# The first mixer's residual: raw rows turned again, or normed rows kept and scaled back

## The chip, the cores and the metric

The kernel runs on one core of a Trainium2 chip. Its engines are TensorE (PE, with its weight loads as PEld), VectorE (DVE), ScalarE (ACT), GpSimd (POOL) and SyncE (SP), which here only issues DMAs. The metric is the device time of one execution in microseconds.

## The reference

The program is one inference step of a two-layer decoder for a prompt of 1024 tokens and 8 single sample tokens, with model width 1024. What matters here is the start of layer 0, for `h = x`:

```python
hn = rmsnorm(h, g[0])                 # y = h * rsqrt(mean(h*h) + EPS), then y * g
mix, S = a_mixer(hn, w_in_a[l], ...)  # gated recurrence and attention into 256 memory tokens
h = h + rmsnorm(mix, g[1])            # the residual: h is still x here
h = h + rmsnorm(swiglu(rmsnorm(h, g[2]), w_gu[l], w_down[l]), g[3])
```

The memory tokens (256 x 1024) are projected to keys and values for both layers, which the attention part of each mixer reads and which are outputs too.

## The kernel before

The kernel works on features in partitions and tokens along the free dimension. The 1024 features are 8 blocks of 128 (`ND = 8`); the tokens are two groups, `g = 0` with 512 prompt tokens and `g = 1` with the other 512 and the 8 sample tokens (520 wide). Every projection (`proj`, matmuls at L220) is an fp32 product made from three fp32r products: weights are loaded by SP (L201), split into a high part on ACT (L206) and a low part on DVE (L207), and multiplied with inputs that were split in the same way. Raw weight tiles have 5 buffers, split ones 5; a projection needs two of each.

**The order of the work.** The code is written as generators. `weave` interleaves several of them by step counts and weights, `drain` runs one to its end; this gives the order in which instructions are written down. A planner then orders each engine's queue by that order and by its own estimate of when operands and buffers are ready. On the chip each engine, and each DMA queue, works through its own list in order: an instruction that waits holds up all behind it.

**Input norm, `start` (L326), called for both groups.** `rms_rows` (L313) takes 128 token rows at a time (tokens in partitions): a sum of squares on ACT or DVE, a logarithm (L320) and an exponential (L321) give `1/rms` per token, and DVE scales the rows in place (L322). Then, for each feature block, PE transposes four 128x128 pieces into one PSUM bank (L349), and ACT and DVE evacuate it into the two parts of the input `x` with the gain column `g[0]` (L352, L353). Even blocks use the bank `ns`, of which there is one, odd blocks `s`, of which there are three. The unscaled rows `x` aren't kept.

**Residual, `residual` (L365).** It adds `h` to the normed mixer output `R`, with DVE's scalar_tensor_tensor (L381) and an add. For later sub-layers `h` comes from a DRAM scratch `hs[g]`, which the residual before it stored at L389. For the first mixer (`first=True`) there is no such store: it loads the raw rows of `x_prompt` again (L372), PE turns them in the bank `ns` (L380), and DVE adds the bank (L383); sample tokens are added from `xsraw` (L385). The first group's residual runs among the second group's projections (`weave` at L1547), the second group's among the heads of layer 1 (L1572).

**The memory tokens, `mem_load` (L798).** Two loads (L803), 16 transposes in the bank `ns` (L807), and copies and subtractions (L227, L228) into the tiles `memt`. `mem_keys` (L824) and `mem_values` (L851) read them. All three are one chain, woven with the first mixer's core (`hgrn_prompt`, first matmuls at L1168) at L1536 to L1539; before that, at L1535, the first mixer's projections for values, gate and queries run alone.

**Small pools.** `T()` gives 128x520 tiles of pool `t`, three buffers, used by the silu, the gate projection, key copies and the masks at the start. `B()` gives 128x512 tiles, seven buffers. A buffer is free again when its last reader has finished; where that is a DMA, when the DMA has landed.

Of the kernel before, what the change touches and what calls it, by code (L numbers as in the profile page):

```python
# [18 lines left out]
P = 128  # L19
# [4 lines left out]
def tile_decoder(  # L24
# [73 lines left out]
    def NS():  # L98
        return nsp.tile([P, 512], F32, tag="ns", name=nm("ns"))
# [74 lines left out]
    def chain(*gens):  # L174
        for g_ in gens:
            yield from g_
# [133 lines left out]
    def wo_tiles(g):  # L310
        return [X(g) for _ in range(ND)]

    def rms_rows(xt, n, dve=False):  # L313
        ss = small([P, 1], tag="rr")
        junk = M().rearrange("p a n -> p (a n)")[:n, :D]
        if dve:
            nc.vector.tensor_tensor_reduce(junk, xt, xt, 1.0, 0.0, ALU.mult, ALU.add, ss[:n])
        else:
            nc.scalar.activation(junk, xt, AF.Square, accum_out=ss[:n])
        nc.scalar.activation(ss[:n], ss[:n], AF.Ln, scale=1.0 / D, bias=epsb[:n])  # L320
        nc.scalar.activation(ss[:n], ss[:n], AF.Exp, scale=-0.5)  # L321
        nc.vector.tensor_scalar(xt, xt, ss[:n], None, op0=ALU.mult)  # L322

# [2 lines left out]
    def start(g, out):  # L326
# [4 lines left out]
            xs = C().rearrange("p a n -> p (a n)")[:NB]  # L331
            nc.sync.dma_start(xs, x_sample.rearrange("b o d -> (b o) d"))
        for tb in range(CH):
            rms_rows(xtok[g][:, tb, :], P, g == 0 and tb % 2 == 1)
            yield
        if g:
            ps = S()
# [8 lines left out]
        for k in range(ND):  # L346
            ps = S() if k % 2 else NS()
            for tb in range(CH):
# [4 lines left out]
            made[0] = nc.vector.scalar_tensor_tensor(  # L353
                x[:, 1, :G], ps, gk, x[:, 0, :G].bitcast(F32), op0=ALU.mult, op1=ALU.subtract
            )
            if g:
                pk = pn[:, k * NB : (k + 1) * NB]
                nc.scalar.activation(x[:, 0, G:], pk, AF.Copy, scale=gk)
                nc.vector.scalar_tensor_tensor(
                    x[:, 1, G:], pk, gk, x[:, 0, G:].bitcast(F32), op0=ALU.mult, op1=ALU.subtract  # L360
                )
# [2 lines left out]

    def residual(g, R, rstd, gc, store, acc=None, first=False):  # L365
        n = NG[g]
        w = D // 2 if first else n
        ht = [xpool.tile([P, 2, w], F32, tag=f"x{g}", name=nm("ht")) for _ in range(ND // 2)]
        for j in range(ND // 2):
            if first:  # L370
                t0 = g * G + j * P
                nc.sync.dma_start(ht[j].rearrange("p a n -> p (a n)"), x_prompt[0, t0 : t0 + P, :])  # L372
            else:
                nc.sync.dma_start(ht[j], hs[g][:, 2 * j : 2 * j + 2, :n])
        for k in range(ND):
            if first:
                ps = NS()
                for tb in range(CH):
                    xf = ht[tb].rearrange("p a n -> p (a n)")
                    nc.tensor.transpose(ps[:, tb * P : (tb + 1) * P], xf[:, k * P : (k + 1) * P], ident)  # L380
            nc.vector.scalar_tensor_tensor(R[k][:, :n], R[k][:, :n], gc(k), rstd[:, :n], op0=ALU.mult, op1=ALU.mult)  # L381
            if first:
                nc.vector.tensor_add(R[k][:, :G], R[k][:, :G], ps)  # L383
                if g:
                    nc.vector.tensor_add(R[k][:, G:n], R[k][:, G:n], xsraw[:, k, :])  # L385
            else:
                nc.vector.tensor_add(R[k][:, :n], R[k][:, :n], ht[k // 2][:, k % 2, :])
            if store:
                nc.sync.dma_start(hs[g][:, k, :n], R[k][:, :n])  # L389
            if acc is not None:  # L390
                sq_acc(acc, R[k][:, :n], k, n)
            yield
# [1082 lines left out]
    with tc.issue_after(made[0].ins):  # L1475
# [56 lines left out]
        nc.gpsimd.tensor_tensor(pidx, pidx, iot, op=ALU.add)  # L1532
    drain(head)
    a0 = mixer_a(0, x0)
    drain(a0.v(), a0.fq())  # L1535
    weave(  # L1536
        (a0.core(), 22),
        (chain(mem_load(), mem_keys(0), mem_values(0), mem_keys(1), mem_values(1), a0.qm(M)), 22),
    )  # L1539
    a0.open()  # L1540
    a1 = mixer_a(1, x1)
# [94 lines left out]
```

## Time and profile before

| | |
|---|---|
| median of 3 runs | 2454.28 us (2452.27 to 2455.25) |
| profiled execution | 2454.5 us |
| its span | 2452.8 us |
| PE busy | 2413.3 us (98%) |
| DVE busy | 1639.9 us (67%) |
| ACT busy | 1252.4 us (51%) |
| POOL busy | 187.0 us (8%) |
| DMA moved | 397.40 MB, 162 GB/s in the mean |

Busy times are sums of instructions' spans with overlaps counted once. In a timeline a row is a run of like instructions: its start, its length, the engine, the line of the code, what it writes and reads, and in brackets how long the engine stood idle before it and what ended that. In a table by stretches each engine's busy time stands with its count of instructions, then the clock granted to PE, the share of time in which the 16 DMA engines were busy, and what they moved.

### The profile page before, as it was taken

The page shows a single profiled execution, that of the slowest core. Times are in us where ns is not written, and L with a number is a line of the kernel's source. Part 1 is how long each engine was busy: PE and PEld are TensorE (multiplying, and loading weights), DVE is VectorE, ACT ScalarE, POOL GpSimd, SP SyncE. Part 2 cuts the span into 40 slices and gives each one's busy share as a digit, 9 for nine tenths or more (in the row PEclk, how much of TensorE's full clock was granted, in tenths as well). Part 3 has the DMA queues.
Part 4 walks back from the last instruction along what each step waited for, and adds up shares of the span by engine and source line. Part 5 has one row for each costly group of instructions (what it writes and reads, how often), then busy time and mean ns, then how long its engine had stood idle before and what let it go on. Part 6 is the DMA issues. An engine that isn't in the chain of part 4 may idle for free.

```text
span 2452.8 us, 42098 instructions
## 1 busy us (share of the span) xinstructions
PE 2413.3 (98%) x15839; PEld 2161.2 (88%) x15839; DVE 1639.9 (67%) x2987; ACT 1252.4 (51%) x2441; POOL 187.0 (8%) x315
## 2 busy tenths in 40 slices
PE   8999999999999999999999999999999999999998
PEld 6888889888879988999999989877777888999998
DVE  5766557665797686664756685788688467755565
ACT  5547644354445554555434554555554445654445
POOL 1000101111000000111200102121000100000000
PEclk9999999999999999999999999999999999999999
DMA  6354676567645447676766649745354563464542
GB/s 190 100 174 110 157 197 161 135 171 204 204 137 166 132 147 235 176 188 161 190 172 168 199 132 291 206 146 154 95 164 120 145 191 116 144 194 141 151 143 74
DMA packets 534733, 397.40 MB, mean 162 GB/s; under 512 B 21325, under 2 KB 473018, under 8 KB 534530
## 3 DMA queue, kind: packets, MB, share of 16 engines
q1 hardware_dynamic: 505346, 315.02, 43.2%
q0 software_dynamic: 29184, 79.70, 14.2%
q8 instruction: 124, 2.03, 0.3%
q14 instruction: 79, 0.65, 0.1%
HBM read 364.81 MB, written 101.14 MB: 190 GB/s over the span
## 4 chain that ended last, share of the span: by engine, by line
PE 84%; DVE 6%; DMA 5%; issue 2%; ACT 2%; POOL 0%; SPq 0%; DVEq 0%; ACTq 0%; POOLq 0%
PE mm L220 44%; PE q L511 13%; PE q L648 9%; PE q L464 3%; PE mm L1042 2%; PE s L1188 1%; DMA c<-in_cache_mem_v 1%; PE s L1385 1%; PE s L906 1%; PE mm L824 1%; PE mm L851 1%; PE q L680 1%; PE s L1351 1%; PE s L875 1%; DVE ws L207 1%
## 5 line engine op out<-in xcount | busy, mean ns | idle before, releaser
L220 PE MATMUL mm<-x,ws 128*128 128x260 f32 (+1 forms) x6240 | 1113.6, 335 | 4.9 <-DVE t L237 1.7
L220 PEld LDWEIGHTS mm<-x,ws 128*128 128x128 f32 x6240 | 941.8, 188 | 125.8 <-issue 2.4
L206 ACT CAST ws<-w 128x512 fp32r<-128x512 f32 (+1 forms) x652 | 382.3, 588 | 489.5 <-PE mm L220 337.0
L207 DVE TENSOR_TENSOR ws<-w,ws 128x512 fp32r<-128x512 f32 (+1 forms) x652 | 418.9, 648 | 246.8 <-ACT ws L206 241.7
L220 PE MATMUL mm<-m,ws 128*128 128x512 f32 (+1 forms) x1344 | 281.8, 361 | 0.1
L220 PEld LDWEIGHTS mm<-m,ws 128*128 128x128 f32 x1344 | 217.9, 189 | 36.8 <-issue 1.0
L648 PE MATMUL q<-m,ws 128*128 128x260 f32 (+1 forms) x1824 | 221.8, 283 | 0.0
L648 PEld LDWEIGHTS q<-m,ws 128*128 128x128 f32 x1824 | 218.9, 188 | 1.2 <-DVE t L534 0.4
L502 DVE TENSOR_TENSOR ws<-w,ws 128x512 fp32r<-128x512 f32 x181 | 124.0, 690 | 86.6 <-ACT ws L501 83.6
L501 ACT CAST ws<-w 128x512 fp32r<-128x512 f32 x181 | 111.8, 621 | 110.2 <-PE q L648 35.6
L511 PE MATMUL q<-x,ws 128*128 128x260 f32 (+1 forms) x1188 | 158.1, 282 | 0.0
L511 PEld LDWEIGHTS q<-x,ws 128*128 128x128 f32 x1188 | 148.7, 188 | 0.0
L511 PE MATMUL q<-y,ws 128*128 128x260 f32 x912 | 119.7, 284 | 0.4 <-ACT q L521 0.3
L511 PEld LDWEIGHTS q<-y,ws 128*128 128x128 f32 x912 | 113.7, 189 | 0.8 <-ACT q L521 0.5
L464 PE MATMUL q<-x,ws 128*128 128x260 f32 (+1 forms) x720 | 91.3, 284 | 0.2 <-DVE r L400 0.2
L464 PEld LDWEIGHTS q<-x,ws 128*128 128x128 f32 x720 | 88.4, 189 | 1.8 <-DVE r L400 0.5
L511 PE MATMUL q<-a,ws 128*128 128x260 f32 (+1 forms) x672 | 87.0, 282 | 0.0
L511 PEld LDWEIGHTS q<-a,ws 128*128 128x128 f32 x672 | 83.2, 188 | 0.0
L657 DVE TENSOR_TENSOR r<-r,q 128x260 f32<-128x260 f32 (+1 forms) x128 | 48.5, 420 | 50.5 <-PE q L648 50.5
L237 DVE TENSOR_SCALAR t<-mm 128x512 f32<-128x512 f32 (+1 forms) x58 | 40.1, 691 | 48.0 <-PE mm L220 47.8
L563 POOL COPY mk<-a 128x1 f32<-128x1 f32 x36 | 21.3, 592 | 645.5 <-ACT a L1241 392.9
L228 DVE TENSOR_TENSOR m<-t,m 128x512 fp32r<-128x512 f32 (+1 forms) x88 | 60.8, 691 | 9.4 <-ACT m L227 8.7
(355 smaller groups left out, 3029.5 us busy)
## 6 DMA issues: line engine op xcount, KB each, us to landing
w<-in_w_gu SPq DMA_DIRECT2D x297, 256.0 KB
w<-in_w_down SPq DMA_DIRECT2D x160, 256.0 KB
wsum<-in_w_gu POOLq DMA_DIRECT2D x72, 512.0 KB, 6.6
w<-wsum SPq DMA_DIRECT2D x104, 256.0 KB
w<-in_w_in_a SPq DMA_DIRECT2D x80, 256.0 KB
w<-in_w_o SPq DMA_DIRECT2D x64, 256.0 KB
wsum<-in_w_gu POOLq DMA_DIRECT2D x24, 640.0 KB, 7.3
wsum<-wsum POOLq DMA_DIRECT2D x24, 512.0 KB, 5.7
```

The source lines that it names most:

```text
L206: nc.scalar.copy(ws[:, 0, :n, :], raw[:, :n, :])
L207: nc.vector.tensor_sub(ws[:, 1, :n, :], raw[:, :n, :], ws[:, 0, :n, :].bitcast(F32))
L220: nc.tensor.matmul(ps[:, a, : PW[g]], wt, xt[k][:, xi, o : o + PW[g]], start=(k == 0 and wi == 0), stop=(k == nk - 1 and wi == 2),)
L228: nc.vector.tensor_sub(dst[1], src, dst[0].bitcast(F32))
L237: nc.vector.tensor_scalar(sv(x, g), pv(ps, g), -44.0, None, op0=ALU.max)
L464: ins = nc.tensor.matmul(pp[a][:, :h], wt, xt[k][:, xi, a * h : (a + 1) * h], start=(k == 0 and wi == 0), stop=(k == ND - 1 and wi == 2),)
L501: nc.scalar.copy(w[:, 0, :], src)
L502: nc.vector.tensor_sub(w[:, 1, :], src, w[:, 0, :].bitcast(F32))
L511: nc.tensor.matmul(ps[:, :h], w[:, wj, k * P : (k + 1) * P], x[:, xi, :], start=(first and k == 0 and wi == 0), stop=(k == 3 and wi == 2), ...
L648: nc.tensor.matmul(pp[a][:, :h], wt, mids[k][:, xi, a * h : (a + 1) * h], start=(k == 0 and wi == 0), stop=(k == nf - 1 and wi == 2),)
L657: nc.vector.tensor_add(d, d, pp[a][:, :h])
L1042: nc.tensor.matmul(pb[i][:, a, :], xt[k][:, xi, c * P : (c + 1) * P], ws[:, s, :], start=(k == 0 and wi == 0), stop=(k == ND - 1 and wi == 2),
```

## The change

The first mixer's residual no longer turns the raw rows. `start` keeps what it has in PSUM anyway, the turned rows scaled by `1/rms` but without the gain: ACT copies each bank to a tile of pool `t` and SP stores it to `hs[g]`. `rms_rows` makes a second exponential with the sign turned, which is `rms` per token, and SP stores that to a new DRAM scratch `inv[g]`. The residual loads `hs[g]` as later residuals do, loads `inv[g]` broadcast over the partitions, multiplies each block by it on DVE, and adds. Sample tokens are added as before. The loads from `x_prompt` and the transposes at L380 are gone.

Besides, `mem_load` is taken out of the chain beside the core and woven with the first mixer's gate and query projections; the weight of the chain that is left goes from 22 to 20.

```diff
-    def rms_rows(xt, n, dve=False):
+    inv = [tc.dram_tile([1, G], F32, name=f"inv{g}") for g in range(2)]
+
+    def rms_rows(xt, n, dve=False, keep=None):
...
         nc.scalar.activation(ss[:n], ss[:n], AF.Ln, scale=1.0 / D, bias=epsb[:n])
+        if keep is not None:
+            si = small([P, 1], tag="ri")
+            nc.scalar.activation(si, ss, AF.Exp, scale=0.5)
+            nc.sync.dma_start(keep, si)
         nc.scalar.activation(ss[:n], ss[:n], AF.Exp, scale=-0.5)
...
         for tb in range(CH):
-            rms_rows(xtok[g][:, tb, :], P, g == 0 and tb % 2 == 1)
+            rms_rows(
+                xtok[g][:, tb, :], P, g == 0 and tb % 2 == 1,
+                inv[g][:, tb * P : (tb + 1) * P].rearrange("o p -> p o"),
+            )
...
                 x[:, 1, :G], ps, gk, x[:, 0, :G].bitcast(F32), op0=ALU.mult, op1=ALU.subtract
             )
+            t = T()
+            nc.scalar.copy(t[:, :G], ps)
+            nc.sync.dma_start(hs[g][:, k, :G], t[:, :G])
...
     def residual(g, R, rstd, gc, store, acc=None, first=False):
         n = NG[g]
-        w = D // 2 if first else n
+        w = G if first else n
         ht = [xpool.tile([P, 2, w], F32, tag=f"x{g}", name=nm("ht")) for _ in range(ND // 2)]
         for j in range(ND // 2):
+            nc.sync.dma_start(ht[j], hs[g][:, 2 * j : 2 * j + 2, :w])
+        if first:
+            iv = B()
+            nc.sync.dma_start(iv, inv[g].rearrange("o n -> (o n)").partition_broadcast(P))
+        for k in range(ND):
+            h = ht[k // 2][:, k % 2, :]
             if first:
-                t0 = g * G + j * P
-                nc.sync.dma_start(ht[j].rearrange("p a n -> p (a n)"), x_prompt[0, t0 : t0 + P, :])
-            else:
-                nc.sync.dma_start(ht[j], hs[g][:, 2 * j : 2 * j + 2, :n])
-        for k in range(ND):
-            if first:
-                ps = NS()
-                for tb in range(CH):
-                    xf = ht[tb].rearrange("p a n -> p (a n)")
-                    nc.tensor.transpose(ps[:, tb * P : (tb + 1) * P], xf[:, k * P : (k + 1) * P], ident)
+                nc.vector.tensor_mul(h, h, iv)
             nc.vector.scalar_tensor_tensor(R[k][:, :n], R[k][:, :n], gc(k), rstd[:, :n], op0=ALU.mult, op1=ALU.mult)
-            if first:
-                nc.vector.tensor_add(R[k][:, :G], R[k][:, :G], ps)
-                if g:
-                    nc.vector.tensor_add(R[k][:, G:n], R[k][:, G:n], xsraw[:, k, :])
-            else:
-                nc.vector.tensor_add(R[k][:, :n], R[k][:, :n], ht[k // 2][:, k % 2, :])
+            nc.vector.tensor_add(R[k][:, :w], R[k][:, :w], h)
+            if first and g:
+                nc.vector.tensor_add(R[k][:, G:n], R[k][:, G:n], xsraw[:, k, :])
...
     a0 = mixer_a(0, x0)
-    drain(a0.v(), a0.fq())
+    drain(a0.v())
+    weave((a0.fq(), 8), (mem_load(), 2))
     weave(
         (a0.core(), 22),
-        (chain(mem_load(), mem_keys(0), mem_values(0), mem_keys(1), mem_values(1), a0.qm(M)), 22),
+        (chain(mem_keys(0), mem_values(0), mem_keys(1), mem_values(1), a0.qm(M)), 20),
     )
```

## The prediction

> **What bounds the kernel now.** I read the page first: the busy shares, then the chain that ended last.
>
> ```profile
> span 2452.8 us, 42098 instructions
> ...
> PE 2413.3 (98%) x15839; PEld 2161.2 (88%) x15839; DVE 1639.9 (67%) x2987; ACT 1252.4 (51%) x2441; POOL 187.0 (8%) x315
> ...
> PE 84%; DVE 6%; DMA 5%; issue 2%; ACT 2%; POOL 0%; SPq 0%; DVEq 0%; ACTq 0%; POOLq 0%
> ```
>
> TensorE is busy 2413.3 of 2452.8 us and carries 84% of the chain. A change can therefore earn in two ways only: it takes instructions out of PE's stream where that stream is dense, or it fills one of the holes, 2452.8 - 2413.3 = 39.5 us in all. Anything added to another engine costs nothing until PE waits for it. The profiled execution took 2454.5 us (span 2452.8 and 1.7 around it), 0.2 above the median of the runs, 2454.28; the sum below is made against 2454.5.
>
> Next I asked for the busy time of each engine in the stretches that the change touches: the first mixer's input norm (two rows), its core's beginning, the second token group's input norm (two rows), and the two residuals (344 to 371, and 960 to 980).
>
> ```profile
> core 0: us, PE busy (x) PEld busy (x) DVE busy (x) ACT busy (x) POOL busy (x), PEclk, DMA share, GB/s
> ...
> 10.00:15.00 5.00, 4.34 (x23) 4.04 (x24) 3.41 (x12) 3.69 (x9) 2.50 (x10) 1.00 0.98 306
> 15.00:20.00 5.00, 4.45 (x25) 3.12 (x24) 5.00 (x15) 3.87 (x8) 0.49 (x3) 1.00 0.43 155
> ...
> 216.00:224.00 8.00, 8.00 (x50) 6.54 (x50) 6.52 (x13) 5.74 (x12) 0.00 (x0) 1.00 0.23 68
> 224.00:232.00 8.00, 7.99 (x65) 7.54 (x64) 7.54 (x16) 7.43 (x18) 1.19 (x4) 1.00 0.24 69
> 344.00:371.00 27.00, 26.98 (x223) 26.14 (x224) 21.48 (x37) 13.71 (x27) 0.00 (x0) 1.00 0.54 167
> ```
>
> ```profile
> 20.00:85.00 65.00, 65.00 (x287) 52.96 (x285) 37.84 (x61) 36.39 (x62) 0.00 (x0) 1.00 0.48 142
> 85.00:95.00 10.00, 6.09 (x30) 5.17 (x29) 7.96 (x22) 5.12 (x16) 0.00 (x0) 0.83 0.10 28
> ...
> 960.00:980.00 20.00, 20.00 (x100) 15.83 (x99) 16.90 (x31) 10.67 (x19) 1.10 (x2) 1.00 1.06 297
> ```
>
> PE is dense in both residuals and from 20 to 85. The one large hole here is 85 to 95: 10.00 - 6.09 = 3.9 us without PE work, at a mean granted clock of 0.83.
>
> **Part 1, the residual's transposes go (gain).** `residual(first=True)` turns raw rows on PE, 4 transposes per feature block, 8 blocks, twice: 64.
>
> ```profile
> L380 PE MATMUL ns<-ident,ht x64: 270/273/329, 343.9 to 974.3; 128*128 128x128 f32 x64
> ```
>
> ```profile
> 355.31 0.60 PE L380 MATMUL ns<-ident,ht 128*128 128x128 f32 x4
> 355.66 4.80 PE L220 MATMUL mm<-x,ws 128*128 128x260 f32 x38
> ...
> 973.94 0.60 PE L380 MATMUL ns<-ident,ht 128*128 128x128 f32 x4
> 974.30 3.25 PE L220 MATMUL mm<-x,ws 128*128 128x512 f32 x13
> ```
>
> One lasts 273 ns, but they overlap. What a group of four displaces is the time from its start to the next projection's first matmul: 0.35 and 0.36 us here. 16 groups x 0.36 = 5.8 us, which I take. The bounds: 0, if the residual becomes limited by DVE instead (part 2), and 64 x 273 ns = 17.5 us if each stood alone. The row is nearest to 5.8, since projections follow without a gap. The Trainium skill, "TensorE: Matmul & The Clock Gate", Part 4: PE-mode transpose, puts a 128x128 transpose at about 275 ns in a kernel's context; the duration agrees with the row of 273, and by that price the sum would gain 17.6 instead of 5.8. That alternative is priced among the rivals from the row alone.
>
> **Part 2, the residual's work on DVE (cost 0).** Per block it gains one multiply of 128x512 with the broadcast inverse; the add reads SBUF instead of PSUM at the same price.
>
> ```profile
> L387 DVE TENSOR_TENSOR r<-r,ht x24: 679/688/695, 862.2 to 2111.2; 128x512 f32<-128x512 f32 x16, 128x520 f32<-128x520 f32 x8
> ```
>
> 8 x 0.69 = 5.5 us a residual. DVE idles 27.00 - 21.48 = 5.5 us from 344 to 371, and the multiplies depend on loads alone, so some can run before the residual's own chain begins at 344. The weight splits queued behind them on DVE have several tiles in hand (five split buffers, two to a projection), so PE should not see it: 0, with 0 to 2 us a residual as bounds. The four loads per residual keep their bytes (512 KB each); they read the scratch `hs` instead of `x_prompt`. Two broadcasts of the inverse are added to SP, under the cover of projections that need no load at that moment.
>
> **Part 3, the memory tokens move (gain).** `mem_load` issues two loads, 16 transposes, 8 ACT copies and 8 DVE subtractions. It moves from the mixer's core into the projections before it.
>
> ```profile
> 84.57 0.60 PE L807 MATMUL ns<-ident,c 128*128 128x128 f32 x4
> 87.77 0.63 PE L807 MATMUL ns<-ident,c 128*128 128x128 f32 x4 [2.60 <-DVE memt L228]
> 89.06 2.93 PE L1168 MATMUL s<-b,a 128*128 128x192 f32 x8 [0.66 <-ACT b L1164]
> 91.78 0.78 PE L807 MATMUL ns<-ident,c 128*128 128x128 f32 x4
> 93.02 0.51 PE L824 MATMUL mm<-memt,ws 128*128 128x256 f32 x2 [0.46 <-ACT memt L227]
> 93.72 1.22 PE L824 MATMUL mm<-memt,ws 128*128 128x256 f32 x8 [0.19 <-DVE memt L228]
> ```
>
> The idle times in the brackets are the hole: 2.60 + 0.66 + 0.46 + 0.19 = 3.9 us. The single bank `ns` makes each group of four wait for the last one's copy and subtraction, and both engines are at the same time on the core's first levels; the memory keys (L824), which are PE's only other work, wait for `memt`. With `memt` ready earlier the keys fill that time. The 16 transposes themselves cost the same in either place. Around them, from 20 to 85, ACT is busy 36.39 of 65 and DVE 37.84, so the moved copies and subtractions are covered by about 27 us of slack on each: 0 there. SP already issues the two loads at 10 us, ahead of everything they could delay:
>
> ```profile
> 10.39 0.91 SPq L803 DMA_DIRECT2D c<-in_mem_prompt  x2
> ```
>  I take the whole 3.9; the bounds are 0 (the hole is the core's own chain) and 3.9.
>
> **Part 4, the first input norm (cost).** Per row block ACT gets one 128x1 exponential and SP one store of 128 single values; per feature block ACT gets one 128x512 copy from PSUM and SP one store of 256 KB.
>
> ```profile
> 8.90 0.20 ACT L321 ACTIVATE rr<-rr 128x1 f32<-128x1 f32 x1
> ...
> 11.92 0.69 ACT L352 ACTIVATE x<-ns,par 128x512 fp32r<-128x512 f32 x1 [0.27 <-PE ns L349]
> ...
> 20.23 0.68 ACT L352 ACTIVATE x<-s,par 128x512 fp32r<-128x512 f32 x1
> ...
> 327.66 0.59 ACT L398 COPY m<-mm 128x512 f32<-128x512 f32 x1 [2.15 <-PE mm L220]
> ```
>
> ```profile
> 19.36 19.71 PE L1042 MATMUL mm<-ws,x 128*128 128x512 f32 x84
> ```
>
> Eight copies are 8 x 0.59 = 4.7 us on ACT. From 10 to 20 ACT has 10.00 - 3.69 - 3.87 = 2.4 us free, and PE is filled to 4.34 and 4.45 of 5. The exponentials lie on the chain to the first transposes: one or two of 0.20 count, 0.3 us. A copy also holds its PSUM bank, and for even blocks that is the single `ns`, so the next blocks come later. But the projection that follows takes 12 matmuls per block at 19.71 / 84 = 0.235 us, 2.8 us a block, while the blocks are now made in (20.23 - 11.92) / 7 = 1.2 us each; only the first two or three can be late. I take 1.2, with bounds 0.2 and 4.7. SP's stores wait for ACT's copies and stand ahead of weight loads; the five raw weight tiles hold that off for a few blocks of 2.8 us.
>
> **Part 5, the second input norm (cost).** The same eight copies, here among the gate's silu and the first projections of the second group. From 216 to 232 ACT is free for 16.00 - 5.74 - 7.43 = 2.8 us, so 4.7 overflows by 1.9. PE starts a projection on a block as soon as that is made, in short runs between the transposes, and can take matmuls of a second projection meanwhile, if its weights are split; that splitting is on ACT too.
>
> ```profile
> 226.13 1.09 PE L220 MATMUL mm<-x,ws 128*128 128x260 f32 x7
> 227.05 0.60 PE L349 MATMUL ns<-ident,xtok 128*128 128x128 f32 x4
> 227.41 1.20 PE L220 MATMUL mm<-x,ws 128*128 128x260 f32 x8
> ```
>
> I take 1.5, with bounds 0 and 4.7. The four exponentials lie under a projection: 0.
>
> **The sum.** 2454.5 - 5.8 - 3.9 + 0 + 1.2 + 1.5 = 2447.5 us, 0.3% under the time before. 0.2%, 4.9 us, is about what a measurement of this kernel can tell from no change.
>
> **Rivals.**
>
> Slower: the `t` slots. The copies go to pool `t`, three buffers, and each is held until its store has landed. Copy 4 waits for slot 1, copy 7 again, so the eight need two holds h; ACT stands at the waiting copy, and behind it in its queue the next block and the weight splits. At the six blocks' own pace, 6 x 1.25 = 7.5 us, nothing is lost; each norm loses 2h - 7.5 beyond. The trace doesn't show a `t` store's landing. The nearest bounds:
>
> ```profile
> 17.98 0.33 SPq L1034 DMA_DIRECT2D w<-in_w_in_a  x1
> ...
> 20.80 0.62 ACT L1036 CAST ws<-w 128x512 fp32r<-128x512 f32 x1
> ```
>
> ```profile
> wsum<-in_w_gu POOLq DMA_DIRECT2D x18, 512.0 KB, 6.2
> ```
>
> A 256 KB load is in use 2.8 us after its issue: h = 0.6 + 2.8 = 3.4, no loss. A transfer of twice the size on POOL's queue lands after 6.2: h = 6.8, 6.1 us lost in each norm, and 2447.5 + 12.2 = 2459.7. It ends slower than before from 2 x (2h - 7.5) = 6.8 on, h = 5.5. Against it: the load is the nearer row, and from 216 on DMA is only 0.23 busy; for it: 0.98 from 10 to 15. The Trainium skill, "DMA: Bandwidth & Descriptors", Anatomy of one DMA, gives about 2.0 us plus bytes over 436 GB/s for a transfer, an estimate of 2.6 us for 256 KB; that too would make this rival harmless, and the load's row agrees with it.
>
> Same: the gains are given back. The hole at 85 stays because DVE, 7.96 of 10 busy, runs the core's own first levels there, and the two norms cost their ACT time at nearly full price: 2454.5 - 5.8 - 1 + 2 + 3 = 2452.7.
>
> Much faster: the transposes cost PE their full duration. Then part 1 earns 64 x 273 ns = 17.5 us and the sum is 2435.8. Against it stand the starts 0.35 us apart per group of four.
>
> **How the numbers follow.** The forecast 0.54 (its own range 2444 to 2450), given back 0.26 (2450 to 2456), `t` slots 0.15 (2457 to 2462), full price of transposes 0.05. Faster by over 0.2%: the forecast without its slowest part, and the last, 0.56. Slower by over 0.2%: 0.15, the `t` slots. The same: the rest, 0.29. The range 2442 to 2457.5 leaves out the full price, most of the `t` slots, and little else. The best of the bounds, 2454.5 - 9.7 = 2444.8 with losses at zero, is inside.
>
> **What would show it.** Right: no transposes in the residual and its projections closing up by 0.36 us a group; from 85 to 95 PE near full with memory keys, at full clock; ACT without waits for a DMA at the new copies; PE's idle time near 10 to 20 up by about 1 us. Wrong: ACT rows at the new copy that wait for a store on `hs`, PE waiting for input blocks at 14 to 30 or at 225 to 240, PE waits on weight splits inside the residuals, or a new hole where the core begins.

## The result and the profile after

The changed kernel is slower: 2477.38 us in the median (2476.06 to 2478.34), against 2455.08 for the kernel before in the same series; the ratio is 1.0091, with a 95% interval of 1.0078 to 1.0104. Forecast were 2447.5 us. The profiled execution took 2478.34 us. The page of the changed kernel, the lines that answer to those of before:

```profile
span 2476.6 us, 42097 instructions
...
PE 2415.2 (98%) x15775; PEld 2160.0 (87%) x15775; DVE 1648.0 (67%) x3003; ACT 1259.2 (51%) x2465; POOL 191.3 (8%) x315
...
PE 83%; DVE 6%; DMA 5%; ACT 3%; issue 2%; POOL 0%; SPq 0%; DVEq 0%; ACTq 0%; POOLq 0%
```

PE has the 64 instructions less, yet its holes grew from 39.5 to 2476.6 - 2415.2 = 61.4 us. To place them, I took landmarks that both kernels have. The rows below are of the view of one line's instructions; the two times after the durations are the first and the last start. First the kernel before:

```profile
L220 PE MATMUL mm<-x,ws x6240: 277/286/802, 38.9 to 2052.4; 128*128 128x260 f32 x107, 128*128 128x512 f32 x88
L339 PE MATMUL s<-ident,c x8: 201/202/223, 216.1 to 216.5; 8*128 8x8 f32 x8
L1022 PE MATMUL s<-ident,t x16: 272/273/329, 346.6 to 368.8; 128*128 128x128 f32 x16
L1188 PE MATMUL s<-a,a x384: 217/263/274, 102.8 to 485.5; 128*126 128x64 f32 x32, 128*124 128x64 f32 x32, 128*120 128x64 f32 x32, 128*112 128x64 f32 x32
L1042 PE MATMUL mm<-ws,x x192: 387/394/502, 14.2 to 941.8; 128*128 128x512 f32 x192
L1351 PE MATMUL s<-a,a x96: 273/539/697, 997.6 to 1831.7; 128*128 128x512 f32 x48, 128*128 128x128 f32 x16, 128*128 128x384 f32 x16, 128*128 128x256 f32 x16
L680 PE MATMUL q<-m,ws x192: 275/283/388, 2415.7 to 2442.9; 128*128 128x264 f32 x96, 128*128 128x256 f32 x96
```

The same instructions in the changed kernel:

```profile
L220 PE MATMUL mm<-x,ws x6240: 277/286/799, 51.4 to 2075.0; 128*128 128x260 f32 x107, 128*128 128x512 f32 x88
L348 PE MATMUL s<-ident,c x8: 201/202/223, 222.1 to 222.6; 8*128 8x8 f32 x8
L1028 PE MATMUL s<-ident,t x16: 272/273/331, 365.6 to 385.1; 128*128 128x128 f32 x16
L1194 PE MATMUL s<-a,a x384: 217/262/273, 115.2 to 501.1; 128*126 128x64 f32 x32, 128*124 128x64 f32 x32, 128*120 128x64 f32 x32, 128*112 128x64 f32 x32
L1048 PE MATMUL mm<-ws,x x192: 387/394/796, 25.6 to 957.5; 128*128 128x512 f32 x192
L1357 PE MATMUL s<-a,a x96: 273/590/847, 1016.4 to 1855.0; 128*128 128x512 f32 x48, 128*128 128x128 f32 x16, 128*128 128x384 f32 x16, 128*128 128x256 f32 x16
L686 PE MATMUL q<-m,ws x192: 274/283/388, 2439.5 to 2466.7; 128*128 128x264 f32 x96, 128*128 128x256 f32 x96
```

The differences of these starts cut the program into stretches. The other columns are runs of the study, told below, cut in the same way. All are us, each from one profiled execution.

| stretch (lines of the kernel before) | before | after | memory move alone | inverse stores alone | copies alone | inverse on chip | own buffers | stores by ACT |
|---|---|---|---|---|---|---|---|---|
| first norm: start to first L220 | 38.9 | 51.4 | 39.0 | 53.6 | 40.2 | 40.7 | 38.9 | 40.1 |
| core with memory: to first L339 | 177.2 | 170.7 | 170.8 | 175.9 | 177.7 | 170.7 | 171.1 | 171.2 |
| second norm: to first L1022 | 130.5 | 143.5 | 130.5 | 136.4 | 139.0 | 137.7 | 130.4 | 130.3 |
| first residual: to last L1188 | 138.9 | 135.5 | 139.0 | 139.0 | 138.9 | 135.3 | 135.5 | 135.4 |
| to last L1042 | 456.3 | 456.4 | 456.9 | 455.1 | 456.4 | 456.8 | 456.4 | 456.4 |
| second residual: to first L1351 | 55.8 | 58.9 | 56.6 | 55.8 | 56.5 | 60.8 | 59.5 | 56.9 |
| rest: to last L680 | 1445.3 | 1450.3 | 1447.1 | 1444.8 | 1447.4 | 1447.0 | 1449.9 | 1449.7 |

The second and third columns give the account: +12.5 at the first norm, -6.5 in the core with the memory tokens, +13.0 at the second norm, -3.4 in the first residual, +0.1, +3.1 in the second residual, +5.0 in the rest, together 23.8. The changed kernel lost 25 us in the two norms, which the forecast had put at 2.7.

**The first norm.** SP's own list in the changed kernel, then ACT's rows, then two rows of the chain of waits (start, length, what):

```profile
6.15 3.29 SPq L326 DMA_DIRECT2D inv<-ri  x3
...
14.12 0.33 SPq L326 DMA_DIRECT2D inv<-ri  x1
14.49 1.85 SPq L1040 DMA_DIRECT2D w<-in_w_in_a  x4
```

```profile
13.89 0.20 ACT L325 ACTIVATE ri<-rr 128x1 f32<-128x1 f32 x1 [2.15 <-DMA inv<-ri]
...
24.97 0.62 ACT L1042 CAST ws<-w 128x512 fp32r<-128x512 f32 x1 [7.09 <-DMA w<-in_w_in_a]
```

```profile
6.15 7.66 DMA inv<-ri
...
14.49 10.46 DMA w<-in_w_in_a
```

The first store of 128 single values takes 7.66 us to land. The fourth needs a value buffer (three exist) and so waits for it; the weight loads stand behind the fourth on SP and go out at 14.49, where before they went out at 7.09:

```profile
7.09 3.25 SPq L1034 DMA_DIRECT2D w<-in_w_in_a  x5
```

Then the load itself takes 10.46 us, against 2.8 for one in the prediction. The stretches of the changed kernel show PE without work from 20 to 25, and what the DMA engines do meanwhile:

```profile
10.00:15.00 5.00, 2.61 (x11) 2.16 (x11) 1.90 (x4) 0.85 (x4) 0.00 (x0) 1.00 0.04 2
15.00:20.00 5.00, 2.23 (x8) 1.43 (x8) 1.96 (x7) 1.96 (x4) 1.02 (x3) 1.00 0.80 41
20.00:25.00 5.00, 0.00 (x0) 0.00 (x0) 0.69 (x3) 0.03 (x1) 2.70 (x8) 1.00 0.48 57
```

From 15 to 20 they are 0.80 busy and move 41 GB/s; in the kernel before, 0.98 busy moved 306 (the row 10 to 15 in the prediction).

**The second norm.** Rows of the chain of the changed kernel, and of the waits from 200 to 262 (engine, line, what it waited for: us in all, times, longest):

```profile
206.42 14.63 DMA w<-in_w_in_a
...
240.91 6.40 DMA hs<-t
```

```profile
DVE t L1081 <- issue: 7.2, 1, 7.2
...
PE s L905 <- DVE b L898: 3.9, 1, 3.9
...
ACT ri L325 <- DMA inv<-ri: 3.7, 1, 3.7
ACT ws L206 <- DMA w<-in_w_in_a: 3.4, 1, 3.4
...
ACT t L366 <- DMA hs<-t: 2.7, 1, 2.7
...
PE s L353 <- DVE c L328: 2.5, 1, 2.5
...
PE mm L220 <- ACT x L370: 2.3, 1, 2.3
```

Two causes stand beside each other. The inverse stores again hold up ACT (3.7) and a weight load (3.4 on ACT, 14.63 us on the chain), and PE waits 2.5. And a store of a copied block lands 6.40 us after it was issued; until then its `t` buffer isn't free, ACT waits 2.7 at the next copy, the gate projection's first step on DVE (L1081), which needs a `t` buffer too, 7.2, and PE 2.3 and 3.9. The view names no releaser for the 7.2 ("issue"); that it is the buffer is read from the code, and with buffers of their own for the copies, below, that wait is gone. Forty microseconds from the start of that norm, first before, then after, show what PE lost:

```profile
216.00:256.00 40.00, 39.76 (x286) 36.53 (x286) 32.48 (x64) 30.20 (x70) 6.91 (x14) 1.00 0.58 140
```

```profile
222.00:262.00 40.00, 31.21 (x193) 27.89 (x193) 24.72 (x48) 27.11 (x58) 6.30 (x13) 0.88 0.68 184
```

PE is idle for 8.8 us instead of 0.2, and the granted clock falls to 0.88 in the mean, which is worth another 0.12 x 40 = 4.8 us. Together they give 13.4, near the 13.0 of the table.

### The profile page after: what moved, and what is told of

It reads as the page before. It is cut to its first block, busy times and chain, and to the rows that moved or that the text cites. A ratio compares the mean times of both kernels' runs of the same rounds, so it can differ in the third digit from the quotient of the medians.

```text
span 2476.6 us, 42097 instructions
## 1 busy us (share of the span) xinstructions
PE 2415.2 (98%) x15775; PEld 2160.0 (87%) x15775; DVE 1648.0 (67%) x3003; ACT 1259.2 (51%) x2465; POOL 191.3 (8%) x315
## 4 chain that ended last, share of the span: by engine, by line
PE 83%; DVE 6%; DMA 5%; ACT 3%; issue 2%; POOL 0%; SPq 0%; DVEq 0%; ACTq 0%; POOLq 0%
PE mm L220 43%; PE q L517 13%; PE q L654 9%; PE q L470 3%; PE mm L1048 2%; PE s L1194 1%; PE s L912 1%; DMA w<-in_w_in_a 1%; PE s L1391 1%; PE mm L830 1%; PE mm L857 1%; PE s L881 1%; PE q L686 1%; PE s L1357 1%; DMA w<-in_w_in_b 1%
## 5 line engine op out<-in xcount | busy, mean ns | idle before, releaser
L220 PE MATMUL mm<-x,ws 128*128 128x260 f32 (+1 forms) x6240 | 1116.1, 336 | 9.4 <-DVE ws L207 2.6
L220 PEld LDWEIGHTS mm<-x,ws 128*128 128x128 f32 x6240 | 944.6, 189 | 132.2 <-DVE ws L207 3.4
L207 DVE TENSOR_TENSOR ws<-w,ws 128x512 fp32r<-128x512 f32 (+1 forms) x652 | 418.8, 648 | 254.8 <-ACT ws L206 250.2
L220 PE MATMUL mm<-m,ws 128*128 128x512 f32 (+1 forms) x1344 | 281.8, 361 | 0.8 <-DVE r L406 0.8
L220 PEld LDWEIGHTS mm<-m,ws 128*128 128x128 f32 x1344 | 217.8, 188 | 37.4 <-DVE r L406 1.2
L569 POOL COPY mk<-m 128x1 f32<-128x1 f32 x54 | 25.3, 468 | 553.5 <-ACT m L227 553.1
```

Source lines behind the costliest of these rows:

```text
L207: nc.vector.tensor_sub(ws[:, 1, :n, :], raw[:, :n, :], ws[:, 0, :n, :].bitcast(F32))
L220: nc.tensor.matmul(ps[:, a, : PW[g]], wt, xt[k][:, xi, o : o + PW[g]], start=(k == 0 and wi == 0), stop=(k == nk - 1 and wi == 2),)
L569: mark = nc.gpsimd.tensor_copy(small([P, 1], tag="mk", bufs=1), now[0])
```

## The experiments

Times and ratios are against runs of the kernel before on the same chip (medians 2457.14, 2456.1, 2455.87 and 2455.28 in the four series). The kernel before itself runs from about 2452 to 2461, so differences of the medians of 2 us mean little.

| run | time, us | ratio to before, 95% interval |
|---|---|---|
| memory move alone | 2451.53 | 0.9977 (0.9967 to 0.9987) |
| inverse stores alone | 2472.18 | 1.0070 (1.0047 to 1.0094) |
| copies alone | 2465.0 | 1.0034 (1.0023 to 1.0045) |
| inverse on chip | 2460.59 | 1.0017 (1.0007 to 1.0027) |
| own buffers | 2455.01 | 0.9996 (0.9982 to 1.0010) |
| no multiply | 2455.33 | 0.9993 (0.9982 to 1.0005) |
| eight value buffers | 2477.8 | 1.0092 (1.0069 to 1.0114) |
| 512 bytes a token | 2458.91 | 1.0009 (0.9999 to 1.0018) |
| values apart | 2459.55 | 1.0013 (1.0003 to 1.0023) |
| stores by ACT, second group | 2450.21 | 0.9976 (0.9966 to 0.9985) |
| inverse stores by POOL | 2472.78 | 1.0069 (1.0055 to 1.0084) |
| stores by ACT, both groups | 2452.24 | 0.9983 (0.9975 to 0.9992) |
| transposes put back | 2454.28 | 1.0003 (0.9992 to 1.0015) |
| one reload | 2448.31 | 0.9973 (0.9962 to 0.9984) |

### The parts by themselves

**Memory move alone**: the kernel before with the moved `mem_load` only.

```diff
-    drain(a0.v(), a0.fq())
+    drain(a0.v())
+    weave((a0.fq(), 8), (mem_load(), 2))
...
-        (chain(mem_load(), mem_keys(0), mem_values(0), mem_keys(1), mem_values(1), a0.qm(M)), 22),
+        (chain(mem_keys(0), mem_values(0), mem_keys(1), mem_values(1), a0.qm(M)), 20),
```

> The kernel before with the memory tokens moved and nothing else. Theory A (the stores of single values of the inverse cost the time) and theory B (the copies, held in three buffers until their stores land, cost it) expect the same: the hole of 3.9 us between 85 and 95 is filled, so some 2451, 3 to 4 us under before. If the move itself costs time, a third theory, it comes out at 2455 or above.

It is faster, by 0.23%, and its stretch with the core is 6.4 us shorter, as in the changed kernel. The hole from 85 to 95 is gone in this run:

```profile
85.00:95.00 10.00, 10.00 (x76) 9.72 (x75) 9.26 (x22) 7.28 (x18) 0.00 (x0) 1.00 0.35 105
```

In the kernel before, that stretch had 3.9 us of idle PE and a clock of 0.83. The idle alone was forecast. The lowered clock, 0.17 x 10 = 1.7 us, comes back with it: 5.6 of the 6.4.

**Inverse stores alone**: the kernel before, with the second exponential and the eight stores, which nobody reads.

```diff
+        if keep is not None:
+            si = small([P, 1], tag="ri")
+            nc.scalar.activation(si, ss, AF.Exp, scale=0.5)
+            nc.sync.dma_start(keep, si)
```

> The kernel before plus the second exponential and the eight stores of 128 single values, which nothing reads; the residual is as before. Theory A: the first weight loads land some 10 us later and the first projection begins at about 25 instead of 14, the second norm loses a few more; 2467 to 2475. Theory B: within 2 us of before.

Eight stores of 512 bytes each cost 15 us. By the table it is 14.7 at the first norm and 5.9 at the second, less some 3 us that the other stretches of this profile are shorter. The first norm repeats that of the changed kernel: the weight loads go out at 14.51, and ACT's first use of a weight is

```profile
26.46 0.62 ACT L1045 CAST ws<-w 128x512 fp32r<-128x512 f32 x1 [9.63 <-DMA w<-in_w_in_a]
```

The clock may be why it loses 14.7 and not 12.5: from 20 to 30 it was 0.50 in this profile and 1.00 in that of the changed kernel, though PE was empty from 20 to 25 in both.

**Copies alone**: the kernel before, with the sixteen copies into `t` and their stores.

```diff
+            t = T()
+            nc.scalar.copy(t[:, :G], ps)
+            nc.sync.dma_start(hs[g][:, k, :G], t[:, :G])
```

> The kernel before plus the sixteen copies from PSUM and their stores of 256 KB, which nothing reads before they are written over; the residual is as before. Theory A: 0 to 6 us slower than before, from ACT's 4.7 us in each norm and some waiting for the t buffers. Theory B: 15 us slower or more.

They cost 1.3 us at the first norm and 8.5 at the second, 8 us in the time. That lies between the ranges of the two theories. The first agrees with the forecast's 1.2, the second doesn't with its 1.5.

**Inverse on chip**: the changed kernel, with the inverse left in SBUF. The residual broadcasts it with four TensorE products of ones and a diagonal.

```diff
-            nc.sync.dma_start(keep, si)
+            nc.scalar.activation(keep, ss, AF.Exp, scale=0.5)
...
+                nc.vector.tensor_scalar(d, ident, inv[g][:, tb : tb + 1], None, op0=ALU.mult)
+                nc.tensor.matmul(pi[:, tb * P : (tb + 1) * P], ones, d, start=True, stop=True)
+            nc.scalar.copy(iv, pi)
```

> The changed kernel with the inverse kept in SBUF as four columns per group, and spread over the partitions in the residual by four products of ones with a diagonal; no store or load of the inverse. Theory A: the loss goes, 2446 to 2456. Theory B: it stays at 2470 or above.

16.8 us of the loss go with the stores, broadcast included; the time lies between the ranges of the two theories, since a second cause is left. What stays is mainly the second norm, +7.2, and the second residual, +5.0 in this profile.

**Own buffers**: that version, with the copies in tiles of other pools, which the norm doesn't wait for, two blocks to a tile.

```diff
-            t = T()
-            nc.scalar.copy(t[:, :G], ps)
+            if k % 2 == 0:
+                kt = A() if k < 4 else M()
+            t = kt[:, k % 2, :G]
+            nc.scalar.copy(t, ps)
```

> As e4_inv_onchip, and the copies go to eight buffers of pools that are idle then (four of pool a, four of pool m) instead of the three of t. Theory A2 (what is left of the loss in the second norm, some 7 us by e4's trace, is the t buffers held until the stores have landed): no wait for a store on hs before the copies or the gate projection, and some 7 us under e4, so 2452 to 2455. Theory B2 (the copies' own time on ACT costs it): within 2 us of e4.

The second norm is back at 130.4 us, as before the change, with the same eight copies on ACT. So the copies' ACT time costs nothing there, and the 7 to 8 us were the `t` buffers, held until their stores had landed.

### Why the small stores are slow

**Eight value buffers**: the changed kernel, with a buffer for each of the eight sets of values, so that no exponential waits for a store.

```diff
-            si = small([P, 1], tag="ri")
+            si = small([P, 1], tag="ri", bufs=8)
```

> The changed kernel with eight buffers instead of three for the stored inverse, so that no exponential waits for a store to land. If the wait for a buffer is the main loss in the norms: ACT's waits of 2.1 and 3.7 us go, the weight loads are issued some 4 us earlier, and the time falls by 8 us or more. If the slow transfers behind the small stores are: the first projection still begins at 20 or later and the time falls by under 5 us.

No gain. The weight loads go out 2 us earlier, at 12.46, and are still first used at 24.17. The buffer wait only lay in the shade of the slow transfers.

**Inverse stores by POOL**: the changed kernel, with the stores issued from another queue.

```diff
-            nc.sync.dma_start(keep, si)
+            nc.gpsimd.dma_start(keep, si)
```

> The changed kernel, with the eight stores of single values issued by POOL's queue and not by SP's. Theory B1 (the block is SP's list: the fourth store waits on it for a free buffer while the weights stand behind): the weight loads are issued at about 7 us, land by 16 us, and the first norm's loss of 12.5 us goes: about 2465 us. Theory B2 (the slow transfers themselves hold the weights up on the DMA engines, whoever issues): the loads are issued early and still land at 20 us or later, and the total stays at 2474 to 2478 us.

SP's list is free now, and the loads go out at 8.33; the chain shows the first landing 9.71 us later, at 18.04:

```profile
8.33 11.43 SPq L1040 DMA_DIRECT2D w<-in_w_in_a  x6
```

```profile
8.33 9.71 DMA w<-in_w_in_a
...
20.87 11.74 DMA hs<-t
```

The first weight is used 7 us earlier than in the changed kernel, at 18.07, yet the first norm takes 52.4 us, no better than 51.4. So the order on SP alone isn't the cause: the weight loads that run beside these stores are slow from whatever queue the stores come, and a 256 KB store of a copied block took 11.74 us there. Both numbers of the second theory were missed by a little: the loads landed before 20, and the total, 2472.8, is below its interval; by the profile the gain lies in later stretches.

**512 bytes a token** and **values apart**: the stores alone, twice changed. In one, each token's value is written 128 times, as a row of 512 bytes. In the other it is still one value of 4 bytes, but each token's goes to a 512-byte row of its own. The edit shown is that of the values apart, against the changed lines of the run with the stores alone; the run with 512 bytes also holds its rows in a tile that isn't reused.

```diff
-    inv = [tc.dram_tile([1, G], F32, name=f"inv{g}") for g in range(2)]
+    inv = [tc.dram_tile([G, P], F32, name=f"inv{g}") for g in range(2)]
...
-                inv[g][:, tb * P : (tb + 1) * P].rearrange("o p -> p o"),
+                inv[g][tb * P : (tb + 1) * P, 0:1],
```

> As e2_inv_only, but each token's inverse is written 128 times, a run of 512 bytes a token instead of 4, and from buffers that are not reused. If the single values make the stores slow: the weight loads land as before and the time is within 3 us of before. If any store to DRAM at this place costs it: near e2, 12 us or more over before.

> The kernel before with the second exponential and the eight stores of 128 single 4-byte values, as in the run with the stores alone, but every token's value goes to a 512-byte row of its own. Nothing reads them. Theory I1 (a transfer of 4 bytes is slow by its size): as slow as with the values side by side, about 2470 us (the run with the values side by side: 2472), the first weights used at about 24 to 27 us. Theory I2 (128 values of 4 bytes wait for each other because they fall into the same few 512-byte rows): near the run with 512 bytes a token, about 2459 us, the first weights used before 19 us.

Both remove most of the loss: 2458.91 and 2459.55 us, 2.8 and 3.7 over before in their series, where the values side by side took 2472.18, 15.0 over. With the values apart, SP's list and ACT's first use of a weight read

```profile
12.81 2.33 SPq L1043 DMA_DIRECT2D w<-in_w_in_a  x5
```

```profile
15.62 0.62 ACT L1045 CAST ws<-w 128x512 fp32r<-128x512 f32 x1 [0.35 <-DMA w<-in_w_in_a]
```

2.8 us from issue to use, as in the kernel before, and the first L220 starts at 42.2 instead of 53.6. The packets are as many and as small as in the slow run (535885, of which 22477 under 512 bytes, on both pages); only their addresses differ. So it isn't the size of 4 bytes that makes the transfer slow, but that 128 of them lie side by side in one 512-byte stretch of DRAM; from what distance on they no longer disturb each other, no run shows. The Trainium skill, "DMA: Bandwidth & Descriptors", Specifications, asks for at least 512 bytes to a transfer for full rate and says that smaller ones become a read and a write back. It spoke against these stores, and the run with 512 bytes a token agrees; but by size alone the values apart would have been as slow, and they were not. That neighbouring values wait for each other's read and write back would fit both; no run shows the inside of it.

### The second residual

DVE's multiplications, the loads and the order on SP were the candidates for the loss there. First the seventy microseconds around it, before and after:

```profile
930.00:1000.00 70.00, 70.00 (x350) 57.46 (x349) 47.91 (x83) 36.49 (x64) 5.32 (x8) 1.00 0.79 227
```

```profile
930.00:1000.00 70.00, 65.26 (x302) 53.09 (x302) 44.29 (x76) 30.18 (x53) 2.87 (x4) 0.98 0.75 223
```

4.7 us of idle PE and 0.02 x 70 = 1.4 us of clock, less the 2.9 that the transposes took: 3.2, against 3.1 in the table. The second window ends before the stretch does; over the stretch itself, 957.5 to 1016.4, the idle is 4.7 too and the clock 0.97, which makes it 3.6. PE's idle time there is two waits, one for the low part of a weight (L207) and one, in the norm that follows the residual, for a sum of squares (L256):

```profile
987.43 6.00 PE L220 MATMUL mm<-x,ws 128*128 128x512 f32 x24 [2.61 <-DVE ws L207]
995.56 0.50 PE L256 MATMUL ns<-n,onesr 128*128 128x512 f32 x1 [2.13 <-ACT n L227]
```

ACT's casts of weights and DVE's subtraction show what held each of them:

```profile
983.93 0.62 ACT L206 CAST ws<-w 128x512 fp32r<-128x512 f32 x1 [1.13 <-PE mm L220]
...
992.96 0.62 ACT L206 CAST ws<-w 128x512 fp32r<-128x512 f32 x1 [2.31 <-DMA w<-in_w_in_b]
```

```profile
986.69 0.68 DVE L207 TENSOR_TENSOR ws<-w,ws 128x512 fp32r<-128x512 f32 x1
```

In the first, the weight had been cast by 984.55, but DVE subtracted only from 986.69 on: it was never idle in between and worked on the residual (a multiplication, the scaling of a block, the running sum of squares and two additions). In the second, ACT stood 2.31 us before a cast whose weight came late, and the residual's squares stood behind that cast in ACT's list. So one of the two waits is DVE's list, and only the other is a late load.

**No multiply**: the version with own buffers, without the sixteen multiplications by the inverse, so that the residual adds the normed rows and not `x`.

```diff
-                nc.vector.tensor_mul(h, h, iv)
```

> As f1_own_buffers, with the multiplication by the inverse left out of the residual, so that the output is not the reference's. Theory A3 (the multiplies overload DVE in the second residual, SP's weight loads stand behind stores that wait for DVE, and PE waits for weights): the second residual gains 5 to 8 us against f1, the waits on weight splits there go. Theory B3 (the loads from hs or something else cost it): within 2 us of f1.

2455.33 against 2455.01, and the stretch 61.8 against 59.5: no gain. The traces show why that doesn't clear the multiplications altogether. PE's wait for the split falls from 2.3 us with own buffers to 1.1, but the wait at the sum of squares grows from 1.2 to 4.1, behind a cast for which ACT waited 4.7 us for its load. The multiplications alone don't make the loss: without them another wait takes its place.

**Stores by ACT**: own buffers, with the residual's stores of the new `h` issued by ACT's queue, for the second group, or for both.

```diff
-                nc.sync.dma_start(hs[g][:, k, :n], R[k][:, :n])
+                (nc.scalar if first and g else nc.sync).dma_start(hs[g][:, k, :n], R[k][:, :n])
```

> The version with the inverse on chip and buffers of their own for the copies (2455.0 us), with one edit: the residual stores of the first mixer's second group are issued by ACT's queue and not by SP's. Theory S1 (the second residual loses because SP's list holds those stores, which wait for DVE's sums, ahead of the weight loads): the stretch from the last row projection to the first matmul after the residual goes from 59.5 back to about 54 to 56 us, the total to about 2450 us. Theory S2 (the DMA engines are full there, whoever issues): the stretch stays at 58 to 62 us and the total within 2 us of 2455.

> As the run with the second group's residual stores on ACT's queue, with the first group's there as well. Theory S1: the second stretch as in that run, the first residual the same as now or up to 2 us better, the total 2448 to 2451 us, faster than both kernels. Theory S2: 2455 us within 2 us. A loss of up to 3 us beside either is possible where ACT, which waits for DVE's sum before each store, comes late with its evacuations; it would show as PE idle behind ACT in the residual stages.

What speaks for the order is SP's list of the changed kernel, where each of these stores waits for a sum of DVE with weight loads behind it:

```profile
981.15 5.96 SPq L395 DMA_DIRECT2D hs<-m  x3
987.44 2.87 SPq L201 DMA_DIRECT2D w<-in_w_in_b  x2
```

In the kernel before they come in ones and twos, between the loads:

```profile
958.94 0.34 SPq L389 DMA_DIRECT2D hs<-m  x1
959.69 0.37 SPq L201 DMA_DIRECT2D w<-in_w_in_b  x1
```

With own buffers and SP's stores, then with ACT's for the second group, the same seventy microseconds:

```profile
930.00:1000.00 70.00, 65.80 (x334) 54.59 (x333) 52.82 (x91) 36.67 (x65) 6.77 (x8) 0.98 0.84 240
```

```profile
930.00:1000.00 70.00, 67.90 (x351) 57.25 (x350) 52.97 (x93) 37.97 (x66) 5.14 (x8) 0.98 0.84 240
```

Idle PE falls from 4.2 to 2.1 us, and the time from 2455.0 to 2450.2. The stretch falls from 59.5 to 56.9, less than the 54 to 56 that I had expected of this theory alone. With both groups' stores on ACT it is 57.5, and 2452.2 us; moving the first group's brings nothing. What goes in both runs is the wait at the sum of squares; the wait for the split on DVE stays, 2.1 and 2.6 us. So the order on SP is probably a part of it, about half of the idle. It isn't more than probable: in profiles of kernels with the new residual that keep the stores on SP and its loads as they are, the stretch lies anywhere from 56.6 (inverse stores by POOL) to 61.8, and the intervals of the ratios, 0.9966 to 0.9985 against 0.9982 to 1.0010 for own buffers, still touch.

**Transposes put back** and **one reload**: own buffers, once with 32 transposes of the identity into a PSUM tile that nobody reads, at their old place, once with one of the second group's four loads, used four times.

```diff
+            if first and g:
+                pt = S()
+                for c in range(CH):
+                    nc.tensor.transpose(pt[:, c * P : (c + 1) * P], ident, ident)
```

```diff
-        for j in range(ND // 2):
+        for j in range(1 if first and g else ND // 2):
             nc.sync.dma_start(ht[j], hs[g][:, 2 * j : 2 * j + 2, :w])
```

> The version with the inverse on chip and buffers of their own for the copies, with 32 TensorE transposes put back into the second group's first residual, four a step as the kernel before had them; they turn the identity into a PSUM tile that nobody reads. In that version the stretch from the last row projection to the first matmul after the residual took 59.5 us, with 4.2 us of PE idle between 960 and 980, against 55.8 us and no idle in the kernel before. Theory C1 (the arrival of the weights sets this stretch, and the transposes were only work in its shade): the stretch stays at 57 to 60 us, PE idle falls to 2 us or less, the total stays at 2455 us within 2.5. Theory C2 (the idle has nothing to do with the missing work): the transposes add their 2.9 us, the stretch is 62 us or more and the total 2458.

> The same version, but the second group's first residual loads one of its four 512 KB tiles and uses it for all four (the output isn't the reference's: 1.5 MB of loads are left out, and the multiplications and additions stay as many). Theory D1 (the DMA engines are full there, share 1.00 to 1.08 for 30 us, and that makes the weights late): PE idle in the stretch falls below 1 us, the stretch to 53 us within 1, the 2.9 us of the transposes less than before's 55.8, and the total to about 2449. Theory D2 (only the order on SP's list, where residual stores stand ahead of weight loads): the stretch stays at 58 us or more.

Put back, the transposes cost no time that can be seen: 2454.28 against 2455.01, though with the intervals of the two ratios their 2.9 us aren't excluded. That is the total that I had given the theory that PE has slack there. But the profile denies its other half: the idle didn't shrink, it is 5.5 us, and the stretch is 65.4 long, more than either theory had. Its waits have changed places again: 1.1 us for splits, and 4.4 at the sum of squares, behind a cast for which ACT waited 5.4 us for its load. With one load instead of four the total is 2448.31, as expected of full DMA engines, yet the stretch is 58.7 with 3.5 us idle, not 53; 3.0 of the idle stand behind a cast whose load came late all the same. By its profile, 4.8 of the 6.8 us that it gains on own buffers lie in the rest, where nothing was edited, so its total proves little for this stretch.

Of this residual the following can be said. No profile with the new residual has a shorter stretch than the kernel before, so on balance taking out the 32 transposes earned nothing there. Seven profiles of kernels with the multiplications and the four loads (the changed kernel, inverse on chip, own buffers, eight value buffers, inverse stores by POOL, and both with stores by ACT) have the wait for a split on DVE, 2.1 to 2.6 us at a time. Where the stores are on SP, a second wait of 1.2 to 2.1 us at the sum of squares comes with it. Neither the multiplications nor the order on SP nor the loads account for it all, and how much of it each one makes stays open.

## Why the prediction was wrong

**Part 4, the first input norm, failed most**: forecast +1.2 with a bound of 4.7, measured +12.5. The step that failed is the one on SP: it counted "one store of 128 single values" per row block, and priced the exponential before it and the copies after it, but not the transfer. No row of before showed such a store, and the bound of 4.7 was made of the copies alone. The copies, which the part did price, measured 1.3 alone. The runs put 14.7 on the stores alone.

**Part 5, the second norm**: forecast +1.5 as ACT time, measured +13.0. The ACT time cost nothing: with own buffers the norm is as fast as before. In its place stand the inverse stores again (5.9 alone; the prediction's "four exponentials" at 0 left their transfer out here too) and the `t` buffers (8.5 alone); together 14.4, so they overlap by about one. The buffers are the rival that was given 0.15, with its mechanism and its place right for this norm and wrong for the first. It turned on the time to land. The load's row, 2.8, was taken as the nearer bound, and POOL's 6.2 as the farther one; 6.40 was measured, and 6.15 in the run with the copies alone. With the rival's own formula, two holds of 0.59 + 6.40 less 7.5 are 6.5 us. The estimate of 2.6 us from the Trainium skill's "DMA: Bandwidth & Descriptors", Anatomy of one DMA, had agreed with the load's row and is far below the store's: the measurement decides. That section's fit is for the path of GpSimd's queue, and these stores went by SP's. That it was a store and not a load isn't the reason: in the run with the inverse stores by POOL, stores of 256 KB from other tiles, elsewhere in the program, landed after 2.1 and 2.4 us in the median, and these after 5.8. Here five of them leave SP within about 6 us, amid weight loads; the DMA engines were 1.04 busy from 235 to 245 in the run with the copies alone. The 0.23 that the prediction set against this rival was read from 216 to 232, and the copies run on to 248.

**Part 3, the memory tokens**: the mechanism was right, the term too small, -3.9 forecast against -6.5 (-6.4 alone). The upper bound was set at the idle time of the hole, although the quoted row had its clock of 0.83 beside it, worth 1.7 more.

**Part 1, the transposes**: 2.9 us a residual were forecast. In the first residual it came out at -3.4, so 0.36 us for a group of four was the right price and the 17.5 of the rival wasn't. In the second it came out at +3.1.

**Part 2, the residual on DVE**: the step that failed is that the splits "have several tiles in hand", so that PE doesn't see DVE's work. It held in the first residual. In the second, PE waited 2.6 us for a split that stood behind the residual's work on DVE, one of the signs that the prediction had named. The total without the multiplications is the same, so 0 was right for them as a sum, but only because another wait took the place of that one. Nor was anything but DVE looked at: the quoted row of the second residual showed the DMA engines at 1.06 of their time, and a late load made the other wait.

**The rest**, +5.0 in the profile after, was in no part, and no run places it. Over the study's profiles it lies between 1444.8 and 1452.6 us, also among kernels with the same code there (1445.2 with 512 bytes a token, 1448.9 with the values apart), so a part of it at least is the scatter of single executions.

The sum fails by 4 and 5 first: 25.5 us against 2.7. Without these stores and with own buffers the same idea takes 2455.0 us, no faster than before, because by the profiles the second residual, and the unplaced rest, give back what the first and the memory move gain. The fastest version of it that computes the whole, the second group's stores on ACT's queue, takes 2450.2 us, 0.24% less than before (0.15 to 0.34) and 1.1% less than the changed kernel. The memory move alone takes 2451.5, about the same. No gain of the kept rows beyond it is shown.

## What to carry to other kernels

Price every new DMA by its landing, and by what runs beside it, not by its bytes or its issue: four stores of 512 bytes, as 128 neighbouring single values each, cost more here than all 64 transposes were worth, and the same values kept in SBUF, or a row apart, cost little. Where a store reads a tile from a small pool, the tile is held until the store lands, and the users of that pool, not only the storing engine, pay for it. When work is taken from a dense stretch, ask what feeds it: here the freed time turned into waits for a weight's split behind other work on DVE and for a weight's load.

## What the runs showed of the hardware

- Single 4-byte values stored side by side to DRAM took 7.66 us to land, and 256 KB loads started beside them 9.7 to 11.9 us instead of 2.8, on another queue as well; the DMA engines were 0.80 busy at 41 GB/s. The same values 512 bytes apart left the loads at 2.8.
- A 256 KB store to DRAM landed after 5.6 to 6.4 us where five left SP within about 6 us amid weight loads, and after 2.1 to 2.4 in the median elsewhere in the same program (the run with the inverse stores by POOL).
- A hole on PE can cost more than its length: the mean granted clock was 0.88 over the 40 us of the second norm with 8.8 us idle, and 0.83 from 85 to 95 before, with 3.9 idle. Idle time plus the missing clock gave 13.4 of 13.0 and 5.6 of 6.4 in these two places. It doesn't always: in the second residual the run with the inverse stores by POOL had 3.8 us idle at a clock of 1.00, and the first norm's empty five microseconds came with 1.00 in the changed kernel and with 0.50 in the run with the stores alone.
